# A seventeenth expert pair for overflowed tokens, and the sums of the experts loaded before the last pair: a hybrid decoder trunk on one core

## The chip, the cores and the metric

The kernel runs on one core of one Trainium2 chip. The metric is the device time of one execution in microseconds (us); the median of three runs of the kernel before is 1382.35 us (1379.83 to 1384.95). One further execution was profiled; all rows below are of that one.

## The reference

The model has two layers over 512 tokens of width 1024, in float32. Each layer has an attention mixer (three kinds of heads behind one input projection), a layer norm, and then a mixture of experts: a token chooses one of four groups, then two of the eight experts in it. The part that this change touches, cut down:

```python
def hier_moe(x, rg_w, rg_b, re_w, re_b, w_gate, w_up, w_down):
    ...
    g_star = jnp.argmax(lg, -1)                     # one group of 4
    top_v, top_i = lax.top_k(le, TOP_K_IN_GROUP)    # two experts of its 8
    w_sel = jax.nn.softmax(top_v, -1)
    gate = (g_hot[:, :, None] * (p_top * gate_e)[:, None, :]).astype(x.dtype)
    for g in range(N_GROUPS):
        h = jax.nn.silu(jnp.einsum('td,edf->tef', t, w_gate[g])) * jnp.einsum('td,edf->tef', t, w_up[g])
        y = y + jnp.einsum('tef,efd->td', h * gate[:, g, :, None], w_down[g])

x = layer_norm(DEEPNORM_ALPHA * x + mix, ln1_g[l], ln1_b[l])
moe = hier_moe(x, ...)
x = layer_norm(DEEPNORM_ALPHA * x + moe, ln2_g[l], ln2_b[l])
```

## The kernel before

A layer's attention ends in the output projection. Its result is normalised to `yn` (without the norm's gain and bias), written to a DRAM tensor `xd` (L920), and the router is computed beside it. `first_rows` (L885 to L890) makes the full norm output, gain and bias from the tile `gb1`, on the vector engine (DVE) and writes it from ACT's queue to a second DRAM tensor `y2`, to which the experts' outputs are then added: `y2` holds the sum that the second norm reads.

There are 32 experts. Each gets 64 slots (`CAP`), and two experts form a pair, so a layer has 16 pairs. `hots` builds one-hot matrices token by slot on DVE, `lists` turns them by matmuls into row numbers and gate weights, `fetch` gathers a pair's 128 token rows from `xd` by an indirect DMA on POOL (L1000; a row number out of range, as empty slots have, is skipped). `turned` transposes the rows on TensorE (PE) and applies gain and bias. `experts_up` (tile `S`) is 32 matmuls, one half of PE's columns for each expert; `experts_mid` makes `h` on ACT and DVE; `experts_down` transposes `h`, multiplies by the down weights into two banks `o`, scales them by the gate, one on ACT (L1044) and one on DVE (L1045), into one of three row buffers, and scatters the 128 rows into `y2` by an indirect DMA that adds (L1046).

An expert's weights are 3.15 MB (two units of 128 rows of 12 KB). `load_next` issues a pair's units on SP's queue in the order of use (L530) into a ring of 13 buffers named by `RING`; it is called six units ahead, and a load waits until the matmuls of the buffer's last use are done.

Tokens beyond 64 of one expert overflow. `pieces` counts, on the chip, how many further pieces of up to 64 tokens there are (`eidi`, `end`, `ni`), at most 16. After the last pair, `overflow` loops over them with `tc.For_i` (L1139), a loop with a count read from memory: it loads one expert's weights, builds the list, gathers, computes and scatters, one piece at a time. All engines enter and leave the loop together.

Then the four tiles of `y2` are loaded (L1251), normalised (L1260 to L1265), and either written out (second layer) or transposed as the next layer's input. The next layer's first input weights are loaded and split into two parts ahead of the loop (L1235; L194 to L199).

The program is written in this order, and a planner puts each engine's instructions into a fixed order from its own estimate of when each is ready; an instruction may be placed ahead of earlier ones of the program that are not ready. The queues run that order.

Of the kernel before, what the change touches and what calls it, by code (L numbers as in the profile page):

```python
# [7 lines left out]
F32 = mybir.dt.float32  # L8
F32R = mybir.dt.float32r
# [7 lines left out]
NT = S // 128  # L17
# [47 lines left out]
def trunk(tc, a, out, dbg=None):  # L65
# [4 lines left out]
    with es:  # L70
# [177 lines left out]
        for l in range(DEPTH):  # L248
# [269 lines left out]

            def load_next(n=1):

                for j in range(units["n"], min(units["n"] + n, NE)):
                    units["n"] += 1
                    p, u = j // 2, j % 2
# [359 lines left out]
            y2 = dr.tile([S, D], F32, name="y2", tag="y2")  # L883
# [19 lines left out]
            for i in range(NT):  # L903
                z = yn[i]
                out_proj(i, 2, 768, 1024)
                if i == 0:
                    zt(NT - 1, 0, 3)
                    zt(NT - 1, 3, 6)
                zt(i, 6, 8)
                V.bn_stats(bst[i][:, 1], z[:, 512:1024])  # L910
                t = bank("S")
                for k in range(NK):
                    mm(t[:, :36], zT[i][:, k], rwg[:, k], k == 0, k == NK - 1)
                mv = norm_scale(bst[i], LN_EPS)
# [6 lines left out]
                if i:  # L921
                    first_rows(i - 1)
# [96 lines left out]

            halves_ = ((0, 64), (64, 128))  # L1020
# [8 lines left out]
            def experts_mid(gu):  # L1029
                h = cp.tile([128, FH], F32, name="h", tag="rwg")  # L1030
                A.activation(h, gu[:, 0:FH], AF.Silu)  # L1031
                V.tensor_tensor(h, h, gu[:, FH:2 * FH], OP.mult)
                return h

            def experts_down(h, w, rows):
                hT = cp.tile([128, 2, 128], F32, name="hT", tag="rw")
                transposes(hT.rearrange("p a b -> p (a b)"), [h[:, 0:128], h[:, 128:256]], 128)
# [5 lines left out]
                y = row_room()  # L1043
                last_on["A"] = A.activation(y[:, 0:512], o[0], AF.Copy, scale=rows[1])  # L1044
                last_on["V"] = V.tensor_scalar(y[:, 512:1024], o[1], rows[1], None, op0=OP.mult)  # L1045
                return G.indirect_dma_start(out=y2, out_offset=bass.IndirectOffsetOnAxis(ap=rows[0], axis=0), in_=y,  # L1046
                                            in_offset=None, bounds_check=S - 1, oob_is_err=False, compute_op=OP.add)

            RI, XR, XG = {}, {}, {}
# [8 lines left out]
            def lists(b, P=None):  # L1058

                Pf = (P or hots(b)).rearrange("p t e s -> p t (e s)")  # L1060
                for q in range(2):
                    t = bank("T")
                    e0 = 4 * b + 2 * q
                    for i in range(NT):
                        mm(t[:, 0:6], Pf[:, i, 128 * q:128 * q + 128], tok[:, i, :, e0:e0 + 2], i == 0, i == NT - 1)
                    rv = small.tile([128, 3], F32, name="rv", tag="rv", bufs=8)
                    V.tensor_copy(rv[0:64], t[0:64, 0:6:2])
                    V.tensor_copy(rv[64:128], t[64:128, 1:6:2])
                    RI[2 * b + q] = slot_rows(rv)

            def fetch(p):
                if p < NE // 2:
                    XR[p] = gathered(RI[p][0])
# [25 lines left out]
            first_rows(NT - 1)  # L1099
# [4 lines left out]
            XG[0] = turned(XR.pop(0))  # L1104
# [6 lines left out]
            eidi, ctr = sm([MAX_ITEMS + 1], "eidi", I32), sm([1], "ctr")  # L1111
            V.tensor_copy(cnt, pos[:, 128:128 + NE])

            def pieces():
# [17 lines left out]
                V.tensor_scalar(eidi[:, :MAX_ITEMS], eid, float(NE - 1), None, op0=OP.min)  # L1132
                V.tensor_copy(eidi[:, MAX_ITEMS:], end[:, NE - 1:NE])
                V.memset(ctr, 0.0)

            def overflow():

                n_items = nc.values_load(eidi[0:1, MAX_ITEMS:MAX_ITEMS + 1], min_val=0, max_val=MAX_ITEMS)
                with tc.For_i(0, n_items) as item:  # L1139
# [66 lines left out]
                    y = row_room()  # L1206
                    A.activation(y[0:64, 0:512], o[0:64], AF.Copy, scale=wr[0:64])
                    V.tensor_scalar(y[0:64, 512:1024], o[64:128], wr[64:128], None, op0=OP.mult)
# [3 lines left out]
            for p in range(NE // 2):  # L1212
# [4 lines left out]
                if p + 1 < NE // 2:  # L1217
                    XG[p + 1] = turned(XR.pop(p + 1))
                    fetch(p + 3)
                if p % 2 == 0 and p // 2 + 2 < NE // 4:  # L1220
                    lists(p // 2 + 2)
                st = experts_down(h, w, RI.pop(p))
                load_next()
                if p % 2:
                    tc.declare_no_dep(st.ins, st0.ins, reason="a token has one group: the two pairs of a batch share no row")
                st0 = st
                if p == 3:
                    pieces()
                    gb2 = norm_rows(1)

            last = l == DEPTH - 1
            with tc.issue_after(last_on["PE"].ins), tc.issue_after(last_on["A"].ins), tc.issue_after(last_on["V"].ins), tc.issue_after(st.ins):
                if not last:
                    raw_room()
                    Wc[l + 1, 0] = load_pair(w_in_src(l + 1, 0), chunks[0][1], "VG")  # L1235
            overflow()


            if not last:
                warm(10)  # L1240
# [3 lines left out]
            yts = []  # L1244
            for j in range(2):
                yu = carve(unit("A", "yt"), 0, [2, D])
                for i in range(2):
                    yts.append(yu[:, i])
                    r = 256 * j + 128 * i
                    for c in halves if r == 0 else [slice(0, 1024)]:  # L1250
                        y2d = SP.dma_start(yu[:, i, c], y2[r:r + 128, c])  # L1251
            if not last:
                with tc.issue_after(y2d.ins):
                    Wc[l + 1, 1] = load_pair(w_in_src(l + 1, 1), chunks[1][1], "VG")
            for i in range(NT):
                z = yts[i]
                src = [z[:, c] for c in halves]
# [4 lines left out]
                for t, c in zip(src, halves):  # L1262
                    V.scalar_tensor_tensor(z[:, c], t, mv[:, 0:1], gb2[:, 0, c], op0=OP.subtract, op1=OP.mult)
                for c in halves if i in (0, 3) else [slice(0, 1024)]:
                    V.scalar_tensor_tensor(z[:, c], z[:, c], mv[:, 2:3], gb2[:, 1, c], op0=OP.mult, op1=OP.add)  # L1265
# [5 lines left out]
                for h in range(2):  # L1271
                    t = bank("T")
                    for j in range(4):
# [3 lines left out]
                          t.rearrange("p (k n) -> p k n", k=4))  # L1277
            moe.__exit__(None, None, None)
# [64 lines left out]
```

## Time and profile before

| what | value |
|---|---|
| median of three runs | 1382.35 us |
| the profiled execution's own time | 1385.0 us |
| its span | 1383.2 us |
| PE busy, share of the span | 1194.4 us, 86% |
| DVE | 696.6 us, 50% |
| ACT | 442.9 us, 32% |
| POOL | 292.5 us, 21% |
| DMA, over the span | 293.81 MB, mean 212 GB/s |

The span is cut into 40 equal slices of 34.6 us. The page's row for the DMA gives the busy share of the 16 engines in tenths:

```profile
DMA  7321440115397999998552224200426899999943
```

The two runs of nines, slices 11 to 18 and 32 to 36, are the experts of the two layers. A group in the lists below shows the engine, the operation, the output and inputs by the program's names, their shape, and the idle time before it with what ended that. L97, L297 and L1011 are helpers that record every matmul and transpose, so tiles (`S`, `o`, `acc`, `T`) tell them apart.

### The profile page before, as it was taken

How to read it: one execution, taken by the hardware profiler on the slowest of the kernel's cores; microseconds unless marked ns; L12 is line 12 of the kernel's file. 1: busy time of each engine (PE TensorE's matmuls, PEld its weight loads, DVE VectorE, ACT ScalarE, POOL GpSimd, SP SyncE). 2: the span in 40 equal slices, each digit the busy share in tenths (PEclk: the TensorE clock that was granted, in tenths of full speed). 3: DMA queues.
4: the chain of work that ended last, by engine and by line, in shares of the span. 5: the costliest groups of instructions: out<-in, count | busy, mean ns of one | idle time of the engine just before them, and what ended most of it. 6: DMA issues, size and time to landing. Idle time of an engine off the chain costs nothing. (4 is left out here: it accounts for less than half of the span.)

```text
span 1383.2 us, 18273 instructions
## 1 busy us (share of the span) xinstructions
PE 1194.4 (86%) x6701; PEld 815.8 (59%) x6708; DVE 696.6 (50%) x1822; ACT 442.9 (32%) x1050; POOL 292.5 (21%) x286
## 2 busy tenths in 40 slices
PE   6989999999939989887599999999996699898860
PEld 6989976668924533222398899666795343332320
DVE  7599638684552422111668892668636333211125
ACT  3362256673102221111235322857611122111100
POOL 5332431201001121100332334230000122111011
PEclk9999999999969999999799999999998799999985
DMA  7321440115397999998552224200426899999943
GB/s 240 116 80 51 128 158 11 36 40 185 118 402 279 400 413 405 409 390 287 166 165 78 65 83 140 98 23 22 156 104 247 347 384 407 409 403 410 356 166 123
DMA packets 63898, 293.81 MB, mean 212 GB/s; under 512 B 16064, under 2 KB 20672, under 8 KB 48192
## 3 DMA queue, kind: packets, MB, share of 16 engines
q1 hardware_dynamic: 52128, 267.43, 50.5%
q0 software_dynamic: 9376, 16.81, 4.9%
q10 hardware_dynamic: 2304, 8.39, 1.5%
q8 instruction: 54, 0.88, 0.3%
q14 instruction: 36, 0.29, 0.1%
HBM read 278.06 MB, written 31.82 MB: 224 GB/s over the span
## 5 line engine op out<-in xcount | busy, mean ns | idle before, releaser
L97 PE MATMUL acc<-U,xh 128*128 128x384 f32 (+1 forms) x1584 | 298.9, 343 | 18.9 <-DVE xh L212 7.0
L97 PEld LDWEIGHTS acc<-U,xh 128*128 128x128 f32 x1584 | 280.5, 193 | 21.9 <-issue 6.9
L97 PE MATMUL S<-w,xg 128*64 128x512 f32 (+1 forms) x968 | 272.0, 608 | 10.6 <-DMA w<-w_e 8.9
L97 PEld LDWEIGHTS S<-w,xg 128*64 128x64 f32 x968 | 83.1, 141 | 138.8 <-issue 112.9
L1017 DVE TENSOR_SCALAR xg<-acc,lv 128x128 f32<-128x128 f32 x128 | 45.8, 404 | 179.6 <-PE S L97 142.9
L97 PE MATMUL o<-w,hT 128*64 128x512 f32 x488 | 125.4, 603 | 5.9 <-ACT hT L90 3.4
L199 POOL TENSOR_TENSOR U<-raw,U 128x768 fp32r<-128x768 f32 (+2 forms) x46 | 90.3, 1967 | 166.9 <-ACT U L196 166.9
L1046 POOL DMA_INDIRECT y<-xroom,ri x32 | 51.4, 1607 | 294.8 <-DVE xroom L1045 180.5
L1031 ACT ACTIVATE h<-S 128x256 f32<-128x256 f32 x32 | 12.3, 383 | 270.6 <-PE S L97 270.6
L196 ACT ACTIVATE U<-raw 128x768 fp32r<-128x768 f32 (+2 forms) x88 | 68.0, 812 | 71.6 <-PE acc L97 43.7
L1045 DVE TENSOR_SCALAR xroom<-o,rv 128x512 f32<-128x512 f32 x32 | 24.0, 751 | 117.7 <-PE o L97 117.7
L97 PEld LDWEIGHTS o<-w,hT 128*64 128x64 f32 x488 | 39.2, 138 | 67.1 <-issue 57.4
L1000 POOL DMA_INDIRECT xroom<-xd,ri x33 | 35.2, 1066 | 180.5 <-PE acc L1011 94.5
L199 DVE TENSOR_TENSOR U<-raw,U 128x768 fp32r<-128x768 f32 (+2 forms) x42 | 52.8, 1260 | 36.5 <-ACT U L196 34.0
L1011 PEld LDWEIGHTS acc<-cst,xroom 128*128 128x128 f32 x256 | 29.4, 147 | 60.6 <-issue 36.0
L90 ACT ACTIVATE uc<-T 128x512 f32<-128x512 f32 (+3 forms) x117 | 51.3, 460 | 40.9 <-PE T L297 39.1
L1015 ACT ACTIVATE xg<-acc,lv 128x128 f32<-128x128 f32 x128 | 48.9, 458 | 45.5 <-PE T L97 35.8
L1011 PE MATMUL acc<-cst,xroom 128*128 128x128 f32 x256 | 43.7, 298 | 22.7 <-DMA xroom<-xd,ri 20.7
L97 PE MATMUL acc<-U,oh 128*128 128x384 f32 (+1 forms) x384 | 63.3, 315 | 0.0
L1044 ACT ACTIVATE xroom<-o,rv 128x512 f32<-128x512 f32 x32 | 22.0, 687 | 111.0 <-PE o L97 111.0
L97 PEld LDWEIGHTS acc<-U,oh 128*128 128x128 f32 x384 | 56.8, 189 | 1.2 <-issue 1.0
L403 DVE MATCH_REPLACE8 uc<-m,uc 128x256 f32<-128x256 f32 (+2 forms) x96 | 51.4, 539 | 0.0
(367 smaller groups left out, 1942.0 us busy)
## 6 DMA issues: line engine op xcount, KB each, us to landing
w<-w_e SPq DMA_DIRECT2D x110, 1536.0 KB
raw<-w_in SPq DMA_DIRECT2D x64, 384.0 KB
xroom<-w_e SPq DMA_DIRECT2D x8, 1536.0 KB
w<-w_e SPq DMA_DIRECT2D x24, 512.0 KB
raw<-w_o SPq DMA_DIRECT2D x16, 384.0 KB
gb<-ln_rows SPq DMA_DIRECT2D x4, 1024.0 KB
xd<-yn ACTq DMA_DIRECT2D x8, 512.0 KB
y<-yn ACTq DMA_DIRECT2D x6, 512.0 KB
```

Source lines behind the costliest of these rows:

```text
L90: A.activation(o, i, AF.Copy, scale=1.0 if scale is None else scale)
L97: return PE.matmul(o, l, r, start=start, stop=stop, skip_group_check=True)
L196: A.activation(hi, r, AF.Copy)
L199: e.tensor_tensor(lo, r, hi.bitcast(F32), OP.subtract)
L403: V.match_replace(out=acc_t[i][:, :n], in_to_replace=m8, in_values=acc_t[i][:, :n], imm_value=TAKEN)
L1000: G.indirect_dma_start(out=xr[0:n], out_offset=None, in_=xd, in_offset=bass.IndirectOffsetOnAxis(ap=ri[0:n], axis=0), bounds_check=S - 1, ...
L1011: PE.transpose(t[:, 128 * j:128 * j + 128], xr[:, 128 * k:128 * k + 128], ident)
L1015: A.activation(xg[:, k], o, AF.Identity, scale=lv[:, 0, k, 0:1], bias=lv[:, 0, k, 1:2])
L1017: V.tensor_scalar(xg[:, k], o, lv[:, 0, k, 0:1], lv[:, 0, k, 1:2], op0=OP.mult, op1=OP.add)
L1044: last_on["A"] = A.activation(y[:, 0:512], o[0], AF.Copy, scale=rows[1])
L1045: last_on["V"] = V.tensor_scalar(y[:, 512:1024], o[1], rows[1], None, op0=OP.mult)
L1046: return G.indirect_dma_start(out=y2, out_offset=bass.IndirectOffsetOnAxis(ap=rows[0], axis=0), in_=y, in_offset=None, bounds_check=S - 1, ...
```

## The change

- `y2` is filled with zeros early in the layer, from one POOL-cleared tile, and `first_rows` goes. In its place `half_rows` makes half of the norm's output for each gathered row (gain and bias in `gb1` are halved by ACT), on DVE, in the row buffer of the pair; the eviction of `o` adds to it, both banks now on DVE. A token has two experts, so the halves make a whole.
- The first two overflowing pieces become a pair of their own, `PX`, the tenth of 17 in `ORDER`. `pieces` (now after the third pair) computes the addresses of their weight rows; where there is no such piece, these lie out of range. The weights are fetched by twelve indirect DMAs on POOL of 128 rows of 4 KB each. `piece_lists` makes the pair's lists on DVE and PE. Its two halves are scattered one after the other. The loop starts at the third piece.
- Ahead of the last pair, `sums` runs the loop and loads the norm's rows and the four tiles of `y2`. The last pair isn't scattered: its rows stay in `y_last`, and matmuls with the transposed one-hot `pT` put them on their tokens in PSUM. In the second layer identity matmuls add the loaded tile there; in the first, DVE adds.
- The next layer's first weights are split on DVE alone, after the last pair's `h`; the copy of `hT` is always on DVE.

```diff
+            PX = NE // 2
+            ORDER = [*range(9), PX, *range(9, PX)]
+            w_rows = a["w_e"].rearrange("l e u p (c f) -> (l e u p c) f", c=3)
...
+                    if p == PX:
+                        for d, e in enumerate(es_):
+                            for c in range(3):
+                                G.indirect_dma_start(out=EW[e][u][:, 1024 * c:1024 * c + 1024], out_offset=None, in_=w_rows,
+                                                     in_offset=bass.IndirectOffsetOnAxis(ap=widx[:, u, c, d:d + 1], axis=0),
+                                                     bounds_check=DEPTH * NE * 768 - 1, oob_is_err=False)
+                        continue
...
+            y2 = dr.tile([S, D], F32, name="y2", tag="y2")
+            none = ring("P")
+            G.memset(none, 0.0)
+            SP.dma_start(y2.rearrange("(p r) c -> p (r c)", r=NT).rearrange("p (n c) -> p n c", c=512), none.unsqueeze(1).to_broadcast([128, 2 * NT, 512]))
...
-            def first_rows(i):
-
-                z = yn[i] if i < NT - 1 else at.tile([128, D], F32, name="x1", tag="u", bufs=3)
-                V.tensor_tensor(z, yn[i], gb1[:, 0], OP.mult)
-                V.tensor_tensor(z, z, gb1[:, 1], OP.add)
-                A.dma_start(y2[128 * i:128 * i + 128, :], z)
-
+            A.activation(gb1.rearrange("p a d -> p (a d)"), gb1.rearrange("p a d -> p (a d)"), AF.Copy, scale=0.5)
...
+            def half_rows(xr, n=128, y=None):
+
+                y = row_room() if y is None else y
+                V.tensor_tensor(y[0:n], xr[0:n], gb1[0:n, 0], OP.mult)
+                V.tensor_tensor(y[0:n], y[0:n], gb1[0:n, 1], OP.add)
+                return y
...
-                last_on["A"] = A.activation(y[:, 0:512], o[0], AF.Copy, scale=rows[1])
-                last_on["V"] = V.tensor_scalar(y[:, 512:1024], o[1], rows[1], None, op0=OP.mult)
+                for n in range(2):
+                    c = slice(512 * n, 512 * n + 512)
+                    last_on["V"] = V.scalar_tensor_tensor(y[:, c], o[n], rows[1], y[:, c], op0=OP.mult, op1=OP.add)
...
+            def sums():
+
+                overflow()
+                yus = [unit("A", "yt") for _ in range(2)]
...
+                        y2d = SP.dma_start(yu[:, i], y2[r:r + 128, :])
...
+            for q, p in enumerate(ORDER):
                 w = (EW.pop(2 * p), EW.pop(2 * p + 1))
+                if p == PL:
+                    gb2, y2d = sums()
                 gu = experts_up(XG.pop(p), w)
                 load_next()
                 h = experts_mid(gu)
+                if p != PL:
+                    p1 = ORDER[q + 1]
+                    XG[p1], HR[p1] = turned(XR[p1]), half_rows(XR.pop(p1), y=y_last if p1 == PL else None)
+                    if q + 3 < n:
+                        fetch(ORDER[q + 3])
...
+                if p == PX:
+
+                    added(y, rows[0], 64)
+                    added(y, second)
+                elif p != PL:
+                    sts[p] = added(y, rows[0])
...
+            for i in range(NT):
+                zb[i] = [bank(("acc", "S", "o")[i % 3]) for _ in halves]
+                for t, c in zip(zb[i], halves):
+                    if last:
+                        mm(t, ident, yts[i][:, c], True, False)
+                    mm(t, pT[:, i], y_last[:, c], not last, True)
```

## Rows read from the trace of the kernel before

**Rows 1.** The page, chain that ended last: shares of the span by line
```profile
PE acc L97 8%; DMA w<-w_e 8%; PE S L97 5%; PE o L97 5%; PE T L297 2%; DMA xroom<-xd,ri 2%; DMA xd<-yn 1%; PE acc L1011 1%; ACT dp L566 1%; PE T L97 0%; ACT uc L90 0%; POOL mv L236 0%; DMA yt<-y 0%; DMA y<-xroom,ri 0%; DVE yt L1265 0%
```

**Rows 2.** Windows, layer two: PE, PEld, DVE, ACT, POOL busy (count); PEclk; DMA; GB/s
```profile
1065.00:1070.00 5.00, 0.00 (x0) 0.00 (x0) 2.27 (x3) 0.00 (x0) 0.00 (x0) 0.50 0.58 235
...
1240.00:1260.00 20.00, 18.35 (x79) 5.84 (x75) 3.05 (x8) 2.60 (x7) 3.69 (x3) 1.00 1.02 409
```

**Rows 3.** Timeline, POOL: gathers early in layer one and midway in layer two
```profile
439.79 1.05 POOL L1000 DMA_INDIRECT xroom<-xd,ri  x1 [3.19 <-PE acc L1011]
...
452.08 1.04 POOL L1000 DMA_INDIRECT xroom<-xd,ri  x1 [3.38 <-PE acc L1011]
...
1213.27 1.04 POOL L1000 DMA_INDIRECT xroom<-xd,ri  x1 [4.86 <-PE acc L1011]
...
1228.14 1.04 POOL L1000 DMA_INDIRECT xroom<-xd,ri  x1 [4.08 <-PE acc L1011]
```

**Rows 4.** Windows, layer one, the start of the experts
```profile
415.00:425.00 10.00, 10.00 (x42) 4.27 (x40) 3.74 (x18) 2.79 (x5) 1.00 (x1) 0.74 0.16 37
```

**Rows 5.** Timeline, all engines, end of layer one
```profile
643.84 1.55 POOL L1046 DMA_INDIRECT y<-xroom,ri  x1 [12.13 <-DVE xroom L1045]
...
653.62 0.34 SPq L352 DMA_DIRECT2D rb<-rb  x1
...
660.88 2.13 POOL L1046 DMA_INDIRECT y<-xroom,ri  x1 [15.48 <-ACT U L196]
...
671.69 0.69 DVE L1260 BATCH_NORM_STATS2 bst<-yt 128x6 f32<-128x512 f32 x1 [2.71 <-DMA yt<-y]
```

**Rows 6.** Timeline, all engines, end of layer two
```profile
1314.94 1.55 POOL L1046 DMA_INDIRECT y<-xroom,ri  x1 [10.90 <-DVE xroom L1045]
...
1318.84 2.74 PE L97 MATMUL S<-w,xg 128*64 128x512 f32 x10
...
1328.68 0.75 DVE L1045 TENSOR_SCALAR xroom<-o,rv 128x512 f32<-128x512 f32 x1 [6.22 <-PE o L97]
...
1359.57 0.69 DVE L1260 BATCH_NORM_STATS2 bst<-yt 128x6 f32<-128x512 f32 x1 [7.63 <-DMA yt<-y]
```

**Rows 7.** Timeline, DVE, layer two before the first gather: start, us, instruction, idle before
```profile
1062.14 0.29 DVE L972 SCALAR_TENSOR_TENSOR posm<-S,selb 128x128 f32<-128x128 f32 x1 [0.60 <-PE S L97]
1067.73 1.22 DVE L888 TENSOR_TENSOR yn<-yn,gb 128x1024 f32<-128x1024 f32 x1 [5.30 <-DMA xd<-yn]
...
1070.35 1.09 DVE L1054 TENSOR_TENSOR oneh<-posm,cst 128x256 fp32r<-128x256 f32 x3
```

**Rows 8.** Chain in order of time, layer two, up to the one-hots: start, us
```profile
1056.13 11.58 DMA xd<-yn
```

**Rows 9.** Timeline, DVE, the same place in layer one
```profile
387.66 1.23 DVE L888 TENSOR_TENSOR yn<-yn,gb 128x1024 f32<-128x1024 f32 x1 [4.74 <-DMA xd<-yn]
```

**Rows 10.** Waits of SP's queue: us in total, times, longest
```profile
SPq L1139 <- DMA y<-xroom,ri: 49.1, 2, 37.9
...
SPq L243 <- DVE yn L889: 14.0, 1, 14.0
```

**Rows 11.** DMA from 1110 to 1160: packets, MB, share of 16 engines; median landing
```profile
q1 hardware_dynamic: 1636, 17.88, 84.8%
q0 software_dynamic: 1152, 2.10, 16.8%
...
xroom<-xd,ri POOLq DMA_INDIRECT x4, 11.8
```

**Rows 12.** DMA from 415 to 425, layer one: median landing
```profile
xroom<-xd,ri POOLq DMA_INDIRECT x1, 3.8
```

**Rows 13.** Timeline, PE, first pairs of layer one
```profile
426.61 1.93 PE L97 MATMUL S<-w,xg 128*64 128x512 f32 x6
428.47 0.44 PE L297 MATMUL T<-cst,h 128*128 128x128 f32 x2
```

**Rows 14.** DMA from 1315 to 1335: packets, MB, share of 16 engines
```profile
q1 hardware_dynamic: 754, 4.84, 60.0%
```

More of the change, by code (lines that the diff above doesn't have):

```diff
@@ L1031, in experts_mid, with experts_down @@
                 A.activation(h, gu[:, 0:FH], AF.Silu)
[L1032 removed]
+                last_on["h"] = V.tensor_tensor(h, h, gu[:, FH:2 * FH], OP.mult)
                 return h
[L1035 removed]
+            def experts_down(h, w, rows, y):
                 hT = cp.tile([128, 2, 128], F32, name="hT", tag="rw")
[L1037 removed]
+                transposes(hT.rearrange("p a b -> p (a b)"), [h[:, 0:128], h[:, 128:256]], 128, None, "V")
+                if w_next:
+                    w_next.pop()()
                 o = [bank("o") for _ in range(2)]
@@ L1103, in trunk @@
             load_next(3)
-            XG[0] = turned(XR.pop(0))
+            XG[0], HR[0] = turned(XR[0]), half_rows(XR.pop(0))
             lists(1)
@@ L1111, in trunk @@
             eidi, ctr = sm([MAX_ITEMS + 1], "eidi", I32), sm([1], "ctr")
+            wbase, widx = sm([2], "wbase"), sm([2, 3, 2], "widx", I32)
+            second = sm([1], "second", I32)
             V.tensor_copy(cnt, pos[:, 128:128 + NE])
@@ L1131, in pieces @@
                     V.tensor_reduce(out=eid[:, i], in_=it, op=OP.add, axis=AX.X)
-                V.tensor_scalar(eidi[:, :MAX_ITEMS], eid, float(NE - 1), None, op0=OP.min)
-                V.tensor_copy(eidi[:, MAX_ITEMS:], end[:, NE - 1:NE])
-                V.memset(ctr, 0.0)
+                V.tensor_scalar(eidi[:, :MAX_ITEMS - 2], eid[:, 2:], float(NE - 1), None, op0=OP.min)
+                V.tensor_scalar(eidi[:, MAX_ITEMS:], end[:, NE - 1:NE], -2.0, 0.0, op0=OP.add, op1=OP.max)
+                V.memset(ctr, 2.0)
@@ new lines, in pieces @@
+                V.memset(second, 4096)
+                V.tensor_scalar(wbase, eid[:, 0:2], NE - 0.5, 2.0 ** 20, op0=OP.is_gt, op1=OP.mult)
+                V.scalar_tensor_tensor(wbase, eid[:, 0:2], 768.0, wbase, op0=OP.mult, op1=OP.add)
+                V.scalar_tensor_tensor(wbase, cc("row")[:, 0:1].to_broadcast([128, 2]), 3.0, wbase, op0=OP.mult, op1=OP.add)
+                for u in range(2):
+                    for c in range(3):
+                        V.tensor_scalar(widx[:, u, c], wbase, float(768 * NE * l + 384 * u + c - 3), None, op0=OP.add)
@@ L1216, in trunk @@
                 h = experts_mid(gu)
[L1217 to L1222, printed above, removed]
-                load_next()
-                if p % 2:
-                    tc.declare_no_dep(st.ins, st0.ins, reason="a token has one group: the two pairs of a batch share no row")
-                st0 = st
@@ L1227, in trunk @@
-                if p == 3:
-                    pieces()
[L1229 to L1236, printed above, removed]
+                if p != PL:
[3 more added lines that the diff above has]
+                        fetch(ORDER[q + 3])
+                elif not last:
+                    raw_room()
+                    w_next.append(next_weights)
@@ new lines, in trunk @@
+                if q + 4 < n:
+                    p4 = ORDER[q + 4]
+                    if p4 == PX:
+                        piece_lists()
+                    elif p4 % 2 == 0:
+                        Pf = lists(p4 // 2)
+                    if p4 == PL - 1:
+                        transposes(pT.rearrange("p a b -> p (a b)"), [Pf[:, i, 128:256].bitcast(F32) for i in range(NT)], 128)
+                rows = RI.pop(p)
+                y = experts_down(h, w, rows, HR.pop(p))
+                load_next()
@@ L1239, in trunk @@
+                if p == PX:
[3 more added lines that the diff above has]
+                    sts[p] = added(y, rows[0])
+                    if p < PL and p % 2:
+                        tc.declare_no_dep(sts[p].ins, sts[p - 1].ins, reason="a token has one group: the two pairs of a batch share no row")
+                if q == 2:
+                    pieces()
             if not last:
-                warm(10)
                 XH[l + 1] = xhp.tile([128, 2, NK, S], F32R, name="xh", tag="xh")
@@ L1243, in trunk @@
             halves = [slice(0, 512), slice(512, 1024)]
[L1244 to L1254, printed above, removed]
+            zb = {}
+            for i in range(NT):
+                zb[i] = [bank(("acc", "S", "o")[i % 3]) for _ in halves]
[3 more added lines that the diff above has]
+                    mm(t, pT[:, i], y_last[:, c], not last, True)
             for i in range(NT):
                 z = yts[i]
-                src = [z[:, c] for c in halves]
+                src = [z[:, c] for c in halves] if not last else zb[i]
+                if not last:
+                    for t, c in zip(zb[i], halves):
+                        V.tensor_tensor(z[:, c], z[:, c], t, OP.add)
                 st = small.tile([128, 2, 6], F32, name="bst", tag="bst", bufs=4)
@@ L1277, in trunk @@
                           t.rearrange("p (k n) -> p k n", k=4))
+                if i == 0:
+                    with tc.issue_after(y2d.ins):
+                        Wc[l + 1, 1] = load_pair(w_in_src(l + 1, 1), chunks[1][1], "VG")
             moe.__exit__(None, None, None)
```

78 lines of the change are left out of this document (60 added, 18 removed).

## The prediction, made before the changed kernel ran

> **What bounds the kernel now.** I read the chain of waits first: two weight-bound stretches, the experts of each layer, show as DMA w<-w_e 8% beside the matmuls that fill between [rows 1]. The windows then say what ends each stretch. Mid-layer the 16 DMA engines are full at 409 GB/s [rows 2], and POOL's gathers, one for each pair of experts, stand 14.87 us apart; early in the layer, with buffers still full, they stand 12.29 us apart, which is what PE needs [rows 3]. So a pair has some 2.6 us of PE slack, 41 us over 16 pairs, and a layer's experts end when the weights have come. Three places break that stream. At the start of the experts the DMA stands idle for want of free buffers (0.16 busy over 10 us in layer one [rows 4], 0.58 over 5 us in layer two [rows 2]) because PE begins late. At the end of layer one, 10.8 us pass between the scatter of the last pair and the first statistics of the norm [rows 5]. At the end of layer two a piece that overflowed 64 slots runs in the loop alone: from the last pair's eviction at 1328.68 to the first statistics at 1359.57 [rows 6]. Layer one runs no iteration. So the trace says how many pieces there are: none, then one.
>
> **Part 1, the start rows of y2 go (first_rows, eight pairs of 1.22 us on DVE, eight writes of 0.5 MB).** In layer two DVE waits 5.30 us for the write of xd, does L888 and L889 and only then finishes the one-hots, at 1071.44 [rows 7]. The positions stand at 1062.43 and have the pair for another tile, 2.4 us, ahead of them. Without all four, positions at 1060.0 and four one-hots (three took 1.09) end at 1061.4: 10 us sooner. What is late next is xd itself, which lands at 1067.7 behind the y2 writes [rows 8]; the gather would go at 1067.5, so it meets the same moment, and there are fewer bytes ahead. In layer one the wait is 4.74 us [rows 9] and four operations of 1.22 lie between: 9 us. The gather's own time stays. Behind SP's load of the second norm rows, which waited 14.0 us for L889, stood weight loads [rows 10]; that load moves to the end. The bytes taken out of the stretch (2 MB and 1 MB) at 409 GB/s are 7.7 us, so the weight stream can keep up with the earlier start. I take -9 and -10; bounds -5 (xd still late) and -13 (DVE freed earlier too). The zeros that replace the rows (2 MB, 5 us) go out in attention, where the page's slices of the DMA are nearly empty; SP waits there for a POOL memset, and behind it stand small transfers of the dilated heads: 0, bounds -1 and +3.
>
> **Part 2, work inside the pairs.** half_rows adds two DVE operations of 1.22 us, and the eviction goes from ACT and DVE to two on DVE: some 3.3 us a pair. DVE is busy 3.05 of 20 us there [rows 2], so it fits, 17 times a layer, at 0. If DVE put half_rows ahead of the copy of hT, PE would lose 2.4 us of its 2.6: still 0, bound +5 a layer. A sum of y now waits longer in its ring of three buffers: half_rows of a pair waits for the scatter three pairs back, and behind it on DVE stand h, hT and the eviction. That matters only if scatters get late (part 4).
>
> **Part 3, the seventeenth pair's own work.** 12.29 us of PE a layer against 41 us of slack: 0. Its weights: nothing in layer one, one expert of 3.15 MB in layer two, +7.7 us at 409 GB/s. That rows out of range move nothing shows already: eight indirect transfers of 128 rows sent 1152 packets but 2.10 MB, 513 rows [rows 11].
>
> **Part 4, how the seventeenth pair's weights come.** Twelve indirect fetches of 128 rows a layer, on POOL 1.04 us each [rows 3], 12.5 us on an engine busy 21% of the span. On the DMA side every row costs a turn, used or not: an indirect transfer is 144 packets, 9 on each engine. Over 50 us the weights' queue took 0.848 x 800 / 1636 = 0.41 us of engine a packet and POOL's queue 0.12 [rows 11]; if they alternate, a POOL packet costs 0.53 us, and twelve fetches 108 x 0.53 = 57 us. They are asked for when pair 6 frees buffers and needed three pairs later, 45 us. Gathers and scatters share that queue, 18 packets or 9.6 us a pair. So they come late, by 12 us if alone and by 41 us with that traffic; the gathers of the next pairs and the scatters stand behind them, and POOL, DVE and PE wait. But meanwhile weights run ahead into the nine of thirteen buffers that are not the seventeenth pair's, 33 us worth; once these are full, POOL's queue has the engines alone, where a gather lands in 3.8 us and not 11.8 [rows 11, 12]. The loss is the time in which no buffer is free, until PE has finished one pair and freed the next: I take 8 us in each layer, nearer to 0 than to the upper bound of 41.
>
> The Trainium skill speaks for less: in "DMA: Bandwidth & Descriptors", "Anatomy of one DMA — SWDGE (gpsimd) path", a fit gives such a transfer 2.0 us plus its bytes at 436 GB/s. By that a fetch of 0.5 MB is 3.2 us, an estimate from that page, and part 4 would cost 0. The trace agrees only where the queue is alone.
>
> **Part 5, the ends.** The loop moves ahead of the last pair. Passing it with no iteration is a full stop: in layer one every engine waits until the scatter has landed [rows 10], part of the 10.8 us after its issue [rows 5]. Now it waits for the scatter of the pair before, and the last pair's scatter is gone: its rows are spread by 128x512 matmuls of pT, which I price like those of S, ten in 2.74 us [rows 6]. What of the last pair's first matmuls goes ahead of the loop decides. In before, work that follows in the program was put ahead of waiting work: next-layer rb on SP before the loop [rows 5], pair 1's first six matmuls before pair 0's transposes [rows 13]. I take it that most of S goes ahead.
> Layer two: the scatter of pair 14 goes out at 1314.94 [rows 6]; 8 to 10 us later the loop passes, at 1324. The last weights would be there: of the 4.84 MB that the weights' queue moved from 1315 to 1335, 3.15 were the overflowed piece's [rows 14]. Then a quarter of S 2, the 7.85 us that pass from the end of S (1321.58) to that of the eviction (1329.43) [rows 6], the second eviction 0.75, pT and identity 1: 1335.5. From the first statistics to the end is 1383.2 - 1359.57 = 23.6, less some 2 of waiting for reloads: 1357 against 1383.2, so -27; bounds -20 (the other 24 matmuls of S, 6.5 us, behind the loop too) and -31.
> Layer one: the scatter of pair 14 goes out at 643.84 [rows 5] and the loop passes 10 us later, at 654; the same steps end at 665, and the sums with PSUM (two of 0.75) bring the first statistics to 667 against 671.69 [rows 5]. Four tiles pay 1.4 us of DVE more each, part of it hidden: -4, bounds +3 and -9.
>
> **The sum**, against the profiled execution's own 1385.0 us: -9 - 10 + 7.7 + 16 - 27 - 4 = -26, 1359. The median of the runs shown is 2.65 lower, so 1356.
>
> **Rivals** (on the median's scale).
> A. The loop holds back all of the last pair. For: the loop is one block, and with late weights nothing is ready sooner. Against: [rows 5, 13]. +6.5 and +7: 1370.
> B. POOL's queue is not late, by luck of the turns or because weights leave gaps. For: 3.8 us alone. Against: 11.8 us beside weights. -16: 1340.
> C. Slower: the backlog on POOL's queue isn't cleared while weights pause; every later gather is late too and PE idles with weights at hand. For: ordinary traffic takes 9.6 of 14.87 us, which leaves a third to clear 57. The other parts sum to -42, so it decides from 21 us a layer; at 31 us: 1402. Against: PE standing still empties the weights' queue.
> D. It doesn't do what it says: rows out of range do move 4 KB each. 9.4 MB more, 23 us: 1379, no change. Against: [rows 11].
>
> **Chances.** Forecast 0.46, A 0.22, B 0.17, C 0.10, D 0.05. Range 1337 to 1377: forecast, A and B with the bounds of parts 1 and 5. A measurement of this kernel tells about 0.5% from no change, 6.9 us: faster 0.84 (forecast, A, B, less a little), same 0.06, slower 0.10.
>
> **What would show it.** Right: pair 0's gather 9 to 10 us sooner in each layer; no y2 writes on ACT's queue; an idle of PE of some 20 us and of the DMA of some 8 at the seventeenth pair; the loop without iteration; statistics within 4 us of the last eviction. Wrong: gathers landing in 4 us beside the fetches (B), late ones to the layer's end (C), first S of the last pair after the loop (A).

## The result, and the profile after

The changed kernel takes 1556.44 us (median of four runs, 1552.39 to 1559.65) beside 1383.65 us for the kernel before on the same chip: a ratio of 1.125, 95% interval 1.121 to 1.129. It is 12.5% slower; the prediction was 1356 us, 2% faster, and its range ended at 1377. The profiled execution has a span of 1557.9 us against 1383.2.

Both spans can be cut at the same marks: the last statistics of a layer's first norm, the first gather, the scatter of pair 14 (the last but one), the first statistics of the second norm, the end.

| stretch (us) | before | after | change | forecast |
|---|---|---|---|---|
| start to the first norm, layer one | 380.5 | 379.9 | -0.6 | 0 |
| first norm to first gather, layer one | 23.2 | 14.4 | -8.8 | -9 |
| experts of layer one: first gather to scatter of pair 14 | 240.1 | 336.5 | +96.4 | +8 |
| scatter of pair 14 to the second norm, layer one | 27.9 | 26.8 | -1.0 | -4 |
| attention of layer two | 382.0 | 387.3 | +5.3 | 0 |
| first norm to first gather, layer two | 23.9 | 16.5 | -7.4 | -10 |
| experts of layer two | 237.4 | 351.4 | +114.0 | +15.7 |
| scatter of pair 14 to the second norm, layer two | 44.6 | 24.9 | -19.8 | -27, with the next line |
| second norm to the end | 23.6 | 20.2 | -3.5 | |

The starts and the ends came near the forecast. The experts, costed at 24 us in all, cost 210.

The page after, part 2 and two groups of part 5 (half_rows is L1030 and L1031, the transposes of h are L297):

```profile
DMA  7322510153888687863723334012378876778633
...
L1030 DVE TENSOR_TENSOR xroom<-xroom,gb 128x1024 f32<-128x1024 f32 x32 | 39.2, 1225 | 259.7 <-DMA y<-xroom,ri 214.8
...
L297 PE MATMUL T<-cst,h 128*128 128x128 f32 x68 | 17.5, 347 | 134.8 <-DVE h L1046 134.8
```

The run of nines over the experts is gone: the stretch that was bound by its weights isn't any more. Windows in the middle of layer two, columns as in [rows 2]:

```profile
1220.00:1240.00 20.00, 14.24 (x58) 5.76 (x58) 13.34 (x62) 1.89 (x5) 2.63 (x2) 0.82 0.70 260
1240.00:1260.00 20.00, 13.86 (x57) 6.24 (x58) 6.87 (x19) 0.26 (x1) 1.59 (x1) 0.74 0.77 301
```

PE is busy 13.86 of 20 us and the DMA moves 301 GB/s, against 18.35 and 409 in [rows 2]. The granted clock of these windows, 0.82 and 0.74, is a mean of stretches at 2.4 and at 1.2 GHz (the row gives 1.00 from 1228 to 1240 us and 0.50 from 1242 to 1250, PE having stood idle since 1236.5): PE now stands idle in every pair. Neither resource that bound the kernel is full, so something waits in a circle. The page names it: DVE stood 214.8 us in front of half_rows for a scatter. The timelines of DVE and of POOL show one turn, the time from one pair's scatter to the next one's (scatter L1065, gather L1007, eviction L1061):

```profile
464.14 1.59 POOL L1065 DMA_INDIRECT y<-xroom,ri  x1 [21.10 <-DVE xroom L1061]
468.57 1.04 POOL L1007 DMA_INDIRECT xroom<-xd,ri  x1 [2.84 <-PE acc L1018]
487.04 1.59 POOL L1065 DMA_INDIRECT y<-xroom,ri  x1 [17.42 <-DVE xroom L1061]
```

```profile
475.38 1.22 DVE L1030 TENSOR_TENSOR xroom<-xroom,gb 128x1024 f32<-128x1024 f32 x1 [8.06 <-DMA y<-xroom,ri]
476.52 0.41 DVE L1046 TENSOR_TENSOR h<-h,S 128x256 f32<-128x256 f32 x1
478.13 0.42 DVE L92 COPY hT<-T 128x256 f32<-128x256 f32 x1
...
485.12 1.64 DVE L1061 SCALAR_TENSOR_TENSOR xroom<-o,rv,xroom 128x512 f32<-128x512 f32 x2 [4.33 <-PE o L97]
```

Read as a chain: scatter issued at 464.14, half_rows freed by its landing at 475.38 (11.2 us), h behind it on DVE (1.1), hT (1.6), the down matmuls and the eviction (7.0), the next scatter at 487.04 (1.9). That is a turn of 22.9 us, where before a pair took 12.29 or 14.87 [rows 3]. And the half_rows at 475.38 isn't that of the next pair. Three half_rows stand ahead of the first h, where the program has one:

```profile
404.43 1.23 DVE L1030 TENSOR_TENSOR xroom<-xroom,gb 128x1024 f32<-128x1024 f32 x1 [6.61 <-DMA xroom<-xd,ri]
...
408.80 1.23 DVE L1030 TENSOR_TENSOR xroom<-xroom,gb 128x1024 f32<-128x1024 f32 x1 [0.61 <-DMA xroom<-xd,ri]
...
411.41 1.22 DVE L1030 TENSOR_TENSOR xroom<-xroom,gb 128x1024 f32<-128x1024 f32 x1
...
416.17 0.42 DVE L1046 TENSOR_TENSOR h<-h,S 128x256 f32<-128x256 f32 x1
```

From then on the planner keeps them two pairs ahead: behind the scatter of pair p stands half_rows of p+3, ahead of h of p+1, and the buffer it writes is the one that this very scatter reads.

### The profile page after: what moved, and what is told of

It reads as the page before. It is cut to its first block, busy times and chain, and to the rows that moved or that the text cites. A ratio compares the mean times of both kernels' runs of the same rounds, so it can differ in the third digit from the quotient of the medians.

```text
span 1557.9 us, 18693 instructions
## 1 busy us (share of the span) xinstructions
PE 1266.6 (81%) x6824; PEld 838.4 (54%) x6824; DVE 806.1 (52%) x2017; ACT 423.0 (27%) x1012; POOL 316.8 (20%) x312
## 3 DMA queue, kind: packets, MB, share of 16 engines
q0 software_dynamic: 13120, 19.45, 5.0%
## 5 line engine op out<-in xcount | busy, mean ns | idle before, releaser
L97 PE MATMUL S<-w,xg 128*64 128x512 f32 x1000 | 298.6, 650 | 35.2 <-DMA w<-w_e,widx 18.2
L1030 DVE TENSOR_TENSOR xroom<-xroom,gb 128x1024 f32<-128x1024 f32 x32 | 39.2, 1225 | 259.7 <-DMA y<-xroom,ri 214.8
L97 PE MATMUL o<-w,hT 128*64 128x512 f32 x512 | 153.0, 690 | 8.4 <-DVE hT L92 8.4
L297 PE MATMUL T<-cst,h 128*128 128x128 f32 x68 | 17.5, 347 | 134.8 <-DVE h L1046 134.8
L1065 POOL DMA_INDIRECT y<-xroom,ri x32 | 51.2, 1600 | 370.2 <-DVE xroom L1061 347.4
L199 POOL TENSOR_TENSOR U<-raw,U 128x768 fp32r<-128x768 f32 (+2 forms) x44 | 85.9, 1956 | 197.8 <-ACT U L196 197.3
L97 PEld LDWEIGHTS o<-w,hT 128*64 128x64 f32 x512 | 45.0, 159 | 96.3 <-issue 78.8
L1061 DVE SCALAR_TENSOR_TENSOR xroom<-o,rv,xroom 128x512 f32<-128x512 f32 x64 | 47.6, 750 | 92.1 <-PE o L97 89.2
L297 PEld LDWEIGHTS T<-cst,h 128*128 128x128 f32 x68 | 8.0, 163 | 154.9 <-DVE h L1046 93.9
L1018 PE MATMUL acc<-cst,xroom 128*128 128x128 f32 x272 | 48.6, 309 | 43.8 <-DMA xroom<-xd,ri 29.0
L1007 POOL DMA_INDIRECT xroom<-xd,ri x34 | 40.6, 1194 | 207.1 <-issue 78.3
```

What stands on the lines that cost most here:

```text
L97: return PE.matmul(o, l, r, start=start, stop=stop, skip_group_check=True)
L199: e.tensor_tensor(lo, r, hi.bitcast(F32), OP.subtract)
L297: PE.transpose(t[:rows, 128 * j:128 * j + 128], b, ident)
L1007: G.indirect_dma_start(out=xr[0:n], out_offset=None, in_=xd, in_offset=bass.IndirectOffsetOnAxis(ap=ri[0:n], axis=0), bounds_check=S - 1, ...
L1018: PE.transpose(t[:, 128 * j:128 * j + 128], xr[:, 128 * k:128 * k + 128], ident)
L1030: V.tensor_tensor(y[0:n], xr[0:n], gb1[0:n, 0], OP.mult)
```

## The experiments

| run | edit, on top of the changed kernel | median us | ratio to before, 95% |
|---|---|---|---|
| half_late | half_rows behind h | 1486.1 | 1.072 (1.068 to 1.075) |
| four_rows | four row buffers for sums, not three | 1522.0 | 1.101 (1.097 to 1.105) |
| no_seventeenth | no seventeenth pair | 1540.6 | 1.112 (1.109 to 1.115) |
| half_late_no_seventeenth | half_late, no seventeenth pair | 1442.3 | 1.040 (1.036 to 1.044) |
| one_ring | half_late, in place, five buffers in one ring | 1448.1 | 1.047 (1.044 to 1.050) |
| one_ring_no_seventeenth | one_ring, no seventeenth pair | 1379.0 | 0.996 (0.994 to 0.998) |
| one_ring_wide | one_ring, fetches of 12 KB rows | 1426.2 | 1.032 (1.029 to 1.037) |
| wide_own_second | one_ring_wide, second in a tile for each layer | 1425.1 | 1.030 (1.028 to 1.032) |
| six_rows_wide | wide_own_second, six buffers | 1390.4 | 1.004 (1.003 to 1.006) |
| six_rows_no_seventeenth | six buffers, no seventeenth pair | 1374.0 | 0.991 (0.989 to 0.993) |
| six_rows_narrow | six_rows_wide with the twelve fetches of the change | 1412.0 | 1.020 (1.017 to 1.023) |
| fetch_first | six_rows_wide, last fetches moved ahead on POOL | 1369.3 | 0.989 (0.987 to 0.992) |

The rows were measured on several chips, each beside the kernel before, whose medians there lay between 1383.2 and 1386.3; a difference of up to 3 us between two rows means nothing. The diffs show only the lines that matter.

**half_late**

```diff
-XG[p1], HR[p1] = turned(XR[p1]), half_rows(XR.pop(p1), ...)
+XG[p1] = turned(XR[p1])
+with tc.issue_after(last_on["h"].ins):
+    HR[p1] = half_rows(XR.pop(p1), ...)
```

> The change as it stands, but half_rows of the next pair is placed on DVE behind h of the current pair; before it stood two pairs ahead, in front of that h. Theory W (half_rows of a pair waits in front of h for the scatter issued one pair earlier to land, so that landing, half_rows, h, the down matmuls, the eviction and the scatter run one after the other): the 244 us that DVE stands ahead of half_rows for a scatter mostly go, the pairs come back to 12 to 16 us, the time falls by 150 to 210 us, to 1345 to 1405. Theory Q (the backlog of the seventeenth pair's fetches on POOL's queue holds up the later gathers and scatters): the order on DVE changes little, 1535 to 1560. Theory H (not the wait but the 2.5 us of half_rows themselves on the way to h): 34 pairs by 2.5 us, at most 80 us less, 1475 or more.

70 us less: more than Q allows, within what H allows and far short of W. DVE's waits for scatters are gone, yet in layer one the scatters of the seventh to the ninth pair still come 24 to 32 us apart.

**four_rows**

```diff
+k = turns["y"] % 4
-return carve(xroom, UNIT + 2 * D + D * (turns["y"] % 3), [D])
+return carve(xroom, UNIT + 2 * D + D * k, [D]) if k < 3 else y_last
```

(y_last is laid out earlier for it.)

> The change as it stands, half_rows still two pairs ahead, but four row buffers in place of three (the tile y_last serves as the fourth). Theory W: half_rows now waits for a scatter issued two pairs earlier, which has landed; same gain as with half_rows placed late, 1345 to 1405. Theory Q: no change, 1535 to 1560. Theory H: no change, 1540 to 1565, since the 2.5 us stay in front of h.

34 us less with half_rows still in front of h: H and Q, which allow nothing, fall; W's size is missed again. Its waits say what took the place (L1031 is its half_rows; total us, times, longest):

```profile
DVE xroom L1031 <- DMA xroom<-xd,ri: 123.7, 15, 19.0
DVE xroom L1031 <- DMA y<-xroom,ri: 73.2, 8, 12.0
```

half_rows now waits mostly for the gather of its own rows, still ahead of an h that needs nothing from it.

**no_seventeenth**

```diff
-ORDER = [*range(9), PX, *range(9, PX)]
+ORDER = [*range(PX)]
...
-V.memset(ctr, 2.0)
+V.memset(ctr, 0.0)
```

> The change as it stands, but without the seventeenth pair: 16 pairs, and the loop (ahead of the last pair) starts at the first overflowing piece, as in the kernel before. half_rows still two pairs ahead, three row buffers. Theory W: the pairs keep their 18 to 24 us; what goes is one turn of some 20 us and some 10 us of late weights in each layer, what comes back is one iteration of the loop in layer two, 25 us: 1510 to 1540. Theory Q: with no fetches on POOL's queue the pairs come back to 12 to 16 us: 1360 to 1400. Theory H: 1500 to 1530.

1540.6, at W's upper end. Without a single fetch of weights on POOL's queue most turns stay at 20 to 25 us, and DVE still stands in front of half_rows for a scatter (total us, times, longest):

```profile
DVE xroom L1030 <- DMA y<-xroom,ri: 245.6, 24, 12.8
```

So Q, which is rival C of the prediction, isn't the cause of most of the loss.

**half_late_no_seventeenth**: both edits.

> half_rows behind h of the current pair, and no seventeenth pair (16 pairs; the loop, ahead of the last pair, starts at the first overflowing piece). Against half_late this shows what the seventeenth pair is worth once the wait is gone. Theory W with the sums of the prediction (a stall of 8 us in each layer and 7.7 us of weights against one iteration of the loop, 27 us): 5 to 20 us slower than half_late, 1355 to 1415. If the fetches cost more than the 8 us in each layer (theory Q, now as a second cost behind W), it is faster than half_late by up to 40 us.

44 us faster than half_late, just beyond the 40 allowed to the second cost, where the prediction's sums had it slower. What the turns wait for now, on POOL (gather L1007, scatter L1065) and on DVE (h L1046, half_rows L1030):

```profile
507.39 1.64 POOL L1007 DMA_INDIRECT xroom<-xd,ri  x1 [16.54 <-issue]
511.79 1.59 POOL L1065 DMA_INDIRECT y<-xroom,ri  x1 [2.77 <-DVE xroom L1061]
532.30 1.64 POOL L1007 DMA_INDIRECT xroom<-xd,ri  x1 [18.92 <-PE T L97]
```

```profile
505.09 0.42 DVE L1046 TENSOR_TENSOR h<-h,S 128x256 f32<-128x256 f32 x1
505.43 1.22 DVE L1030 TENSOR_TENSOR xroom<-xroom,gb 128x1024 f32<-128x1024 f32 x1
...
530.00 0.42 DVE L1046 TENSOR_TENSOR h<-h,S 128x256 f32<-128x256 f32 x1
530.34 1.22 DVE L1030 TENSOR_TENSOR xroom<-xroom,gb 128x1024 f32<-128x1024 f32 x1
```

The gathered rows lie in two buffers. Before the change the transposes alone read them; now half_rows reads them too, so the gather at 507.39 goes 2 us after a half_rows that stands behind h. Placed early, half_rows waits for a scatter; placed late, a gather waits for half_rows. Either way a landing of some 10 us becomes part of a turn: here from the seventh pair on, with 22 to 26 us for three pairs; the first six still come 10 to 15 us apart. (The expectation of one_ring gives the gathers of this trace as half_late's.)

**one_ring**: half_rows works in place, and gathered rows and sums share the five buffers.

```diff
-xr = carve(xroom, UNIT + D * (turns["x"] % 2), [D])
+xr = carve(xroom, UNIT + D * (turns["x"] % 5), [D])
...
-y = row_room() if y is None else y
+y = xr if y is None else y
```

> half_rows behind h as in half_late, and it now works in place: the gathered rows, their half, the sum and the scatter share one ring of five row buffers, where before two held gathered rows and three held sums. In half_late the gather of a pair went out only behind half_rows of the pair that held its buffer (gathers at 507.4, 532.3, 556.4 in its trace, each 2 us behind h), and the transposes waited for the landing 10 us later. Theory B (row buffers: whichever ring is short, a landing of 10 us enters each pair's turn): with five buffers the gather goes ahead of h, the pairs come to 12 to 16 us from the fifth on, 1370 to 1420. Theory P (PE's order: transposes of the pair after next stand ahead of the matmuls of the next pair, whatever the buffers): turns of 24 us stay, 1470 to 1490. Theory L (a transfer on POOL's queue takes 10 us beside weights and that alone sets the turn): also 1470 or more.

1448.1: 108 us less than the change, and the turns are 13 to 17 us as B has it, except around the seventeenth pair (22 and 32 us in layer one), which keeps the sum above B's 1420.

**one_ring_no_seventeenth**

> one_ring without the seventeenth pair (16 pairs, loop ahead of the last pair from the first overflowing piece). Theory B: 1370 to 1400, near the kernel before, with layer two's single iteration still in it; the seventeenth pair then costs what one_ring is above this (44 us with the waits in place; by the prediction it gains 5 to 20). Theory P and L: about 1430 to 1445, as with half_late.

1379.0, as B has it, and no turn above 17.4 us up to pair 14. So the loss falls into two costs: row buffers (with half_rows' place among them), and here 69 us for the seventeenth pair. On POOL and PE of one_ring (gather L1003, scatter L1061, fetch of weights L535; the six fetches run to 545.50):

```profile
522.67 2.54 POOL L1061 DMA_INDIRECT y<-xroom,ri  x1 [0.30 <-DVE h L1042]
535.72 1.03 POOL L1003 DMA_INDIRECT xroom<-xd,ri  x1 [10.51 <-DMA y<-xroom,ri]
537.06 1.59 POOL L1061 DMA_INDIRECT y<-xroom,ri  x1 [0.31 <-issue]
538.96 1.05 POOL L535 DMA_INDIRECT w<-w_e,widx  x1 [0.30 <-issue]
...
545.50 0.99 POOL L535 DMA_INDIRECT w<-w_e,widx  x1 [0.30 <-issue]
```

```profile
550.62 6.64 PE L97 MATMUL S<-w,xg 128*64 128x512 f32 x16 [14.26 <-DMA w<-w_e,widx]
```

PE stands 14.26 us for weights that are asked for late. Meanwhile no buffer comes free (SP's queue waits 32.4 us for PE's `o`) and the weights' own queue stops: the DMA's share from 540 to 560 us is 0.48.

**one_ring_wide**: rows of 12 KB, so four fetches a layer in place of twelve.

```diff
-w_rows = a["w_e"].rearrange("l e u p (c f) -> (l e u p c) f", c=3)
+w_rows = a["w_e"].rearrange("l e u p f -> (l e u p) f")
...
-for c in range(3):
-    G.indirect_dma_start(out=EW[e][u][:, 1024 * c:1024 * c + 1024], ...)
+G.indirect_dma_start(out=EW[e][u], ...)
```

> one_ring, with the weights of the seventeenth pair fetched in four indirect DMAs of 128 rows of 12 KB in place of twelve of 4 KB: same bytes, a third of the rows. By part 4 of the prediction (a packet of POOL's queue costs a turn of the engine beside the weights' queue, used or not) 72 of 108 packets on each engine go, 38 of 57 us: the late weights of the seventeenth pair go and it is 10 to 30 us faster than one_ring. If the stall comes from elsewhere (DVE's lists, buffers that come free late), within 5 us of one_ring.

22 us less: the number of rows and of transfers counts, not their bytes. In layer one, where no row is in range and the fetches move nothing, the experts alone (first gather to scatter of pair 14) take 271.7 us in place of 282.6.

**wide_own_second**

```diff
-second = sm([1], "second", I32)
+second = sm([1], f"second{l}", I32)
```

> one_ring_wide, with a tile of its own for the row numbers named second in each layer. In one_ring's trace the memset that prepares second for layer two stands on DVE in layer one, at 602.70, and waits there for the second scatter of the seventeenth pair; DVE does nothing from 585.9 to 602.7. Theory M (this wait delays the evictions and h of the next pairs): 8 to 14 us faster than one_ring_wide, all of it in layer one. Rival: those pairs wait for weights anyway, since the DMA fell behind at the seventeenth pair: within 3 us.

1.1 us, no difference: the rival. In one_ring DVE did stand idle for 16.77 us, up to the memset of the next layer and the operation beside it at 602.7; with the edit that idle is gone, and the time stays. What stood behind it would have been late anyway: a long idle in front of an instruction is no price.

**six_rows_wide**: y_last is the sixth buffer (laid out earlier; ahead of the loop a turn of the ring that would fall on it is skipped).

```diff
+k = turns["x"] % 6
-xr = carve(xroom, UNIT + D * (turns["x"] % 5), [D])
+xr = carve(xroom, UNIT + D * k, [D]) if k < 5 else y_last
```

> wide_own_second with a ring of six row buffers (y_last is the sixth). In one_ring POOL stood until 535.0 in front of a gather, whose buffer the scatter issued at 522.7 still held, and the seventeenth pair's last fetches, whose buffers PE had freed at 528.7, stood behind it. Theory B2 (that order, not the bytes, makes the weights late): the fetches go out 6 to 10 us sooner in each layer and the ordinary pairs lose their waits too: 15 to 30 us faster than wide_own_second. Rival (the fetches are late by their own turns on the DMA engines): 0 to 8 us, from the ordinary pairs only.

35 us less, past B2's upper end.

**six_rows_no_seventeenth**

> one_ring_no_seventeenth with six row buffers. If the gathers' wait for the scatter before still costs the ordinary pairs something: 3 to 12 us faster, 1367 to 1376. If these pairs are bound by their weights: the same, 1376 to 1382.

5 us less than with five, so most of the 35 belong to the seventeenth pair, which still costs 16 us. POOL in six_rows_wide (fetch L534), and PE:

```profile
511.15 1.60 POOL L1061 DMA_INDIRECT y<-xroom,ri  x1 [1.24 <-DVE rv L1083]
526.49 1.03 POOL L1003 DMA_INDIRECT xroom<-xd,ri  x1 [13.73 <-DVE xroom L1057]
527.83 1.61 POOL L1061 DMA_INDIRECT y<-xroom,ri  x1 [0.31 <-issue]
529.75 1.03 POOL L534 DMA_INDIRECT w<-w_e,widx  x1 [0.30 <-issue]
531.09 1.00 POOL L534 DMA_INDIRECT w<-w_e,widx  x1 [0.31 <-issue]
```

```profile
544.99 1.94 PE L97 MATMUL S<-w,xg 128*64 128x512 f32 x2 [11.71 <-DMA w<-w_e,widx]
```

The gather at 526.49 is that of the thirteenth pair, six ahead: the planner puts a gather forward as far as the ring has buffers, and there it blocks POOL until the scatter of 511.15, whose buffer it takes, has landed.

**six_rows_narrow**

> six_rows_wide with the twelve fetches of 4 KB rows, as in the change. If each packet of POOL's queue costs its turn, as part 4 of the prediction had it, the ring of six leaves the 22 us that the wide fetches saved in one_ring: 1408 to 1415. If those 22 us came from POOL's queue standing behind late gathers, which the ring of six has already taken away: 1390 to 1400.

1412.0: the 22 us are there again, with six buffers as with five. Twelve fetches in place of four put more packets on POOL's queue, and they also cost POOL eight more issues of some 1.3 us in each layer. The traces show the packets at work: the scatter behind the first fetches of layer one takes 23.9 us from issue to landing (at 512.16, behind six fetches) against 14.6 in six_rows_wide (at 511.15, behind two), and POOL issues nothing in that time. What POOL's own issuing adds wasn't separated.

**fetch_first**: the scatter of the eighth pair and the gathers written from then on are placed behind the fetches.

```diff
+last_on["px"] = G.indirect_dma_start(out=EW[e][u], ...)
...
+with tc.issue_after(last_on["px"].ins) if q > 6 else ExitStack():
     fetch(ORDER[q + 3])
...
+with tc.issue_after(last_on["px"].ins) if q == 7 else ExitStack():
     sts[p] = added(y, rows[0])
```

> six_rows_wide, with the last two fetches of the seventeenth pair ahead of the eighth scatter and of the gathers on POOL's queue. In six_rows_wide they went out at 529.75 and 531.09, behind a gather that had waited until 526.49 for a scatter to land, though PE had freed their buffers at 510; they landed at 545 and PE had stood 11.7 us for them. Theory B2 (their place in the queue makes them late): they go out near 513 and land before 531, the stall of PE goes in both layers, and of the 16 us that the seventeenth pair still costs against six_rows_no_seventeenth 15 to 30 go: 1360 to 1376. Rival (a fetch beside the weights' queue is late whenever it is issued, or the weights missed at the start of the experts come back as a wait elsewhere): 0 to 8 us faster than six_rows_wide, 1382 to 1391.

1369.3, as B2 has it, and 1.1% below the kernel before (0.987 to 0.992). POOL, and the windows around the pair (columns as in [rows 2]), first in fetch_first, then in six_rows_wide:

```profile
506.28 1.62 POOL L1061 DMA_INDIRECT y<-xroom,ri  x1 [7.38 <-DVE rv L1083]
508.20 1.04 POOL L534 DMA_INDIRECT w<-w_e,widx  x1 [0.30 <-DMA xroom<-w_e]
509.55 0.99 POOL L534 DMA_INDIRECT w<-w_e,widx  x1 [0.31 <-issue]
510.84 0.99 POOL L1003 DMA_INDIRECT xroom<-xd,ri  x1 [0.30 <-issue]
```

```profile
520.00:540.00 20.00, 19.05 (x95) 6.87 (x89) 5.97 (x11) 1.12 (x3) 5.29 (x4) 1.00 1.02 410
540.00:560.00 20.00, 20.00 (x98) 7.96 (x99) 12.17 (x35) 3.04 (x9) 3.50 (x3) 1.00 1.01 411
```

```profile
520.00:540.00 20.00, 12.99 (x56) 4.44 (x56) 7.77 (x13) 2.01 (x6) 4.68 (x4) 0.93 1.01 402
540.00:560.00 20.00, 15.02 (x53) 4.63 (x54) 2.56 (x5) 0.23 (x1) 1.61 (x1) 0.72 0.48 181
```

The fetches go 21 us sooner, no idle of PE is left for them, the DMA stays full and the granted clock is 1.00.

So the distance from 1369 to 1556 us is closed step by step: 21 us for the fetches' place on POOL (fetch_first to six_rows_wide), 22 for their small rows (to six_rows_narrow), 144 (of 187) for row buffers and for half_rows' place among them (to the change; this last step also holds the tile for second).

## Why the prediction was wrong

**The step that failed is in part 2**: half_rows "17 times a layer, at 0", because its wait "matters only if scatters get late". The buffer and the queue were named rightly: half_rows of a pair does wait for the scatter three pairs back, and h, hT and the eviction do stand behind it. What was wrong is which pair's h that is. In the program half_rows of pair 5 stands behind h of pair 4; in DVE's queue it stood, at 475.38, ahead of h of pair 3. It needs only gathered rows and a free buffer, so the planner moved it up; the three buffers then held no slack, and the scatter awaited was the last one issued. A scatter that landed in 11.2 us, not late at all, made that turn 22.9 us long, and the experts, costed at 24 us, lost 210, most of it in such turns. The text did ask what happens if DVE puts half_rows ahead of work that doesn't need it, but priced that by the 2.4 us that half_rows works and not by its wait; and for the ends the same prediction used that the planner puts ready work ahead of waiting work. The front had the numbers to see the cost: a landing of 10 us or more beside weights [rows 11], inside a turn of 12.29 to 14.87 us [rows 3] with 2.6 us of slack.

**The same step forgot a buffer.** It counted the sums' ring but not that half_rows becomes a second reader of the gathered rows. half_late_no_seventeenth shows that cost without the other two: it takes 63 us more than one_ring_no_seventeenth.

**Rival C** had the sign and a landing in each turn, but the wrong place: 1402 us by a backlog of the fetches, while no_seventeenth keeps nearly all of the loss. With 0.10 for all slower cases and a range to 1377, no room was left for a wait that the text itself had written down and set to 0.

**Part 4** was mis-sized in its value, not in its mechanism. It took 8 us a layer between 0 and 41; removing small rows and late place gained 43 us in both layers, 21 a layer, halfway. PE's idle for late weights was forecast as some 20 us a layer; it was 18.2 in both layers together in the changed kernel and 14.26 in layer one of one_ring. The DMA's was forecast as some 8, and one_ring's share of 0.48 over 20 us is 10. That rows out of range still cost their turn, its argument against B and for the forecast, is what the 22 us of one_ring_wide and of six_rows_narrow bear out: 72 of 108 packets an engine taken away in each layer, 11 us gained, 0.15 us of the kernel's time each. On the queue itself the scatter's 9.3 us in six_rows_narrow, behind four fetches or 36 packets an engine more, are 0.26 us each, half the 0.53 of the estimate. What it didn't have is POOL's order: a gather that waits for a landing blocks fetches whose buffers are free.

The Trainium skill's fit ("DMA: Bandwidth & Descriptors", "Anatomy of one DMA — SWDGE (gpsimd) path") gives a fetch that moves nothing 2.0 us, its fixed part. In layer one, which has no overflowed piece, the four fetches of six_rows_wide took from issue to landing (min, median, max):

```profile
DMA to landing us min/median/max: 15.1/16.1/17.2
```

The measurement decides: beside a full weights' queue, and with a scatter or gather ahead of them on POOL's own, the fit doesn't hold.

**Part 1** came out inside its bounds of -5 to -13: first norm to first gather -8.8 and -7.4 us (forecast -9 and -10); the first gather of layer one goes at 394.34. **D** is out: POOL's queue moved 19.45 MB in the changed kernel and 16.29 in one_ring_no_seventeenth, so the 24 fetches brought 3.16 MB, one expert, where all rows would have been 12.6.

**Part 5** was near, by rival A's mechanism. All engines, end of layer two:

```profile
1512.86 1.55 POOL L1065 DMA_INDIRECT y<-xroom,ri  x1 [10.84 <-DVEq L1201]
...
1520.32 8.89 PE L97 MATMUL S<-w,xg 128*64 128x512 f32 x32 [8.54 <-issue]
...
1537.74 0.70 DVE L1355 BATCH_NORM_STATS2 bst<-acc 128x6 f32<-128x512 f32 x1 [1.15 <-PE acc L97]
```

All 32 matmuls of the last pair's S stand behind the loop (in layer one at 738.17 as well), not a quarter of them; but the loop passes 7.5 us after the scatter's issue and not 9, so that -23.2 came of -27, and -1.0 of -4. (By its own figures, 1357 against 1383.2, the -27 is -26.)

**What fetch_first says of the rest.** With room in the ring, large rows and the fetches ahead, it takes 1369.3 us: inside the range of 1337 to 1377, 13 us above the forecast. Of the 14 us that it gains on the kernel before, some 5 are the seventeenth pair's (six_rows_no_seventeenth takes 1374.0).

**What stays open**: the 5.3 us that attention of layer two takes longer. The nine profiled runs with the seventeenth pair take 384.8 to 387.3 us for this stretch, the kernel before and the four runs without the pair 379.4 to 382.5. Between fetch_first and six_rows_no_seventeenth the delay is 0.1 us at 206 us into the stretch and 5.1 at 249; what causes it there wasn't tested.

## What to carry to other kernels

Where a change lets an instruction write or read a buffer that a DMA also holds, count for each such buffer how many turns lie between release and next use in the order that the queues run, not in the order of the program; if an instruction can move up, its wait moves up with it, and stands in front of work that needs none of it. Give a ring so many buffers that the landing time is shorter than the turns between a buffer's release and its next use, and work in place where one tile serves two readers. On a queue that issues DMAs in order, put transfers whose buffers are free ahead of those that wait for a landing, and make few large rows of them.

## What the runs showed of the hardware that was not expected

Indirect fetches of 128 rows with nothing to move take no less time to land beside a full weights' queue than gathers that do move rows: a median of 16.1 us in layer one of six_rows_wide, behind a scatter on POOL's queue, against the 11.8 of the gathers in [rows 11], where eight transfers moved 2.10 MB, some 0.26 MB each.
